# Hymba layer on one core: feed-forward columns interleaved with the output projection, and its input transposed two tiles later

## The chip, the cores and the metric

One core of one Trainium2 chip runs the whole layer in one launch. The metric is the device time of that launch in microseconds (us), as a median of repeated executions. The engines are named as the profile names them: PE (TensorE, matmuls; PEld its weight loads), DVE (VectorE), ACT (ScalarE), POOL (GpSimd) and SP (SyncE, which here only issues DMAs; SPq in the rows). SBUF is the on-chip memory, PSUM holds matmul results, tiles have 128 partitions.

## The reference, cut to what matters

One encoder layer over 2048 positions of width 1024, all in float32. An attention of 8 heads x 64 and a gated unit of 8 groups x 64 read the same normalised input; their outputs stand side by side and go through one output projection. Then comes a feed-forward of hidden width 4096. This part of it is what the change touches:

```python
attn = dilated_attention(q, k, v, rel_bias).reshape(B, S, D_ATTN)
sgu = spatial_gating(jax.nn.gelu(zu), jax.nn.gelu(zv), sgu_ln_g, sgu_ln_b, sgu_w, sgu_b)
mix = jnp.concatenate([attn, sgu], axis=-1) @ w_out
x = x + rms_norm(mix, g_post_mix)
h = rms_norm(x, g_pre_ffn)
f = jnp.square(jax.nn.relu(h @ w_ff1)) @ w_ff2
return x + rms_norm(f, g_post_ffn)
```

## The kernel before

**Precision.** Every matmul operand is split into a high and a low part of a faster float format (the high part by a cast on ACT, the low one as a difference on DVE: `split_sbuf`, L59 and L60, with a scale L56 and L57), and `mm3` makes three matmuls of each product (L84 to L86). So a product of 128x128 by 128x512 is three PE instructions, and each loaded weight costs an ACT and a DVE pass. `piece` loads a 128x512 block of weights on SP's queue into `wraw` and splits it.

**Stages.** Stage 1 (to about 450 us) makes the input projection and the gated unit's inputs. Stage 2 (to about 950 us) is attention, in steps over heads and groups. PE has gaps there, and a generator `gate()` fills them with other work, the *filler*: the rest of the gated unit, and then the half of the output projection that needs only that unit. The filler's results are copied from PSUM to `ot` on ACT (L710) and stored to DRAM as `part`. A plan spreads it: PRE is how much of it (in modelled nanoseconds of PE time) runs ahead of the first step, POST how much stays behind the last, the rest goes in proportion to what the steps leave free. At its last tile the filler loads and splits the eight pieces `c.wo` of `w_out` that the other half of the projection needs. The last `values` of attention are added to DRAM (`od`) by POOL's queue, and a head's denominators are stored as `rd`. At the stage's end the PE and ACT order is pinned to the order in which the code was written (`in_order`); on the other engines a scheduler may move instructions.

**Stage 3** has three loops.
- The output projection, over 16 tiles of 128 positions. `operand(i)` loads `fa` from `od` (L892) and `fr` from `rd` (L895, two loads), multiplies them on POOL (L898) and splits the product into `mh` and `ml`. `rest(i)` loads `r` from `part` (L905) and `xt` from `x` (L907). PE makes 2 x 4 x 3 = 24 matmuls into two PSUM tiles `mo`, DVE adds them to `r` (L936). `post` is a norm and the residual: Square on ACT with a sum (`jk`, L851), two POOL steps for the root (L90, L91), DVE times `gmix` (L912), DVE plus `xt` (L913), a store of `r` to `x1d` on ACT's queue (L914). For the first eight tiles `prep`, one tile behind, norms the new `r` again: Square, two POOL steps, a scaling in place on ACT (L863), eight PE transposes `tp` (L870), and the split of `tp` into `hh` and `hl` (L75, L76). Operands are made two tiles ahead, `rest` one; `r` has three buffers, `xt` two.
- The feed-forward, over two halves of 8 tiles and 8 groups of 512 hidden columns each: `ff1` makes 192 matmuls `f` (4 columns blocks of 128, 8 blocks of the inner dimension, 2 halves of 512 positions, 3 for the precision), Relu on ACT, the square on POOL, a split to `fh` and `fl`; `ff2` makes 192 matmuls `g`, whose sums go to `acc`. The first group's weights are loaded in the last projection tile.
- The output, after the last group of a half: the final norm with `gpost`, the residual from `x1d`, the store.

Memory is handed out in pools, from the left and from the right side of SBUF. A pool that is opened after another one was closed gets its addresses, and its first writers wait for the last readers and writers of what lay there.

## Time and profile before

| | us |
|---|---|
| median of 3 runs | 2513.27 |
| lowest, highest | 2506.41, 2519.23 |
| profiled execution | 2515.86 |
| its span | 2514.0 |
| PE busy in the span | 2390.3 (95%) |
| DVE busy | 1063.1 (42%) |
| ACT busy | 934.9 (37%) |
| POOL busy | 471.2 (19%) |

The span is what the profile shows, from the first instruction to the last; the execution is longer by what lies around it. Busy shares are means over all stages. The page's slices cut the span in 40 equal parts of 62.9 us; each digit is the busy share in tenths, and the row of PE reads `7999999988899996799999999999999999999998`. Slices 16 and 17 (6 and 7, about 943 to 1069 us) are where stage 2 ends and the projection runs. In rows of the timeline the brackets say how long the engine was idle before the instruction and what released it.

### The profile page before, as it was taken

The numbers are of one execution on the slowest core, as the hardware profiler recorded it, in microseconds if no ns is written. First come the engines' busy times: TensorE is split into PE (matmuls) and PEld (weight loads), VectorE is DVE, ScalarE is ACT, GpSimd is POOL, SyncE is SP. The second block draws the span as 40 slices with busy tenths as digits, with TensorE's granted clock in tenths as the row PEclk, the third lists the DMA queues.
The fourth block names the chain that finished last, engine by engine and source line by source line (L and its number), as shares of the span: only waits on it lengthen the run. The fifth ranks groups of instructions, "written<-read, shape, count | busy, mean of one in ns | idle before, by whom it ended". The sixth has DMA issues, their size and how long they took to land.

```text
span 2514.0 us, 31489 instructions
## 1 busy us (share of the span) xinstructions
PE 2390.3 (95%) x11591; PEld 2000.0 (80%) x11591; DVE 1063.1 (42%) x2246; ACT 934.9 (37%) x2053; POOL 471.2 (19%) x521
## 2 busy tenths in 40 slices
PE   7999999988899996799999999999999999999998
PEld 6787888878788885678888888888788888888887
DVE  5433523566766644551322322333722333233226
ACT  4424322366766673433221221123533122212213
POOL 4103103533222222420100110011211001001101
PEclk9999999989999998899999999999999999999999
DMA  7646365878777567761111111111611121111113
GB/s 269 215 138 201 130 189 159 203 175 195 202 175 173 142 153 204 231 232 59 51 47 38 56 47 49 51 51 59 201 59 51 34 67 46 48 42 51 51 43 125
DMA packets 222077, 296.13 MB, mean 118 GB/s; under 512 B 37089, under 2 KB 128740, under 8 KB 218852
## 3 DMA queue, kind: packets, MB, share of 16 engines
q1 hardware_dynamic: 214724, 273.15, 37.4%
q10 hardware_dynamic: 4640, 16.79, 1.7%
q0 software_dynamic: 2560, 4.20, 1.2%
q8 instruction: 91, 1.49, 0.2%
q14 instruction: 62, 0.51, 0.1%
HBM read 216.04 MB, written 82.74 MB: 119 GB/s over the span
## 4 chain that ended last, share of the span: by engine, by line
PE 75%; DMA 12%; DVE 4%; ACT 3%; issue 1%; POOL 1%; SPq 1%; DVEq 0%; ACTq 0%; POOLq 0%
PE f L84 10%; PE f L85 10%; PE f L86 10%; PE g L86 8%; PE g L84 8%; PE g L85 8%; PE mm L84 4%; PE mm L86 4%; PE mm L85 4%; DMA v<-vd 2%; DMA r<-part 2%; PE t L588 2%; PE o L617 1%; PE o L616 1%; PE s L508 1%
## 5 line engine op out<-in xcount | busy, mean ns | idle before, releaser
L85 PE MATMUL f<-hh,wl 128*128 128x512 f32 x1024 | 399.4, 390 | 2.2 <-DVE wl L57 2.2
L86 PE MATMUL f<-hh,wh 128*128 128x512 f32 x1024 | 399.4, 390 | 0.0
L84 PE MATMUL g<-wl,fh 128*128 128x512 f32 x1024 | 399.4, 390 | 0.0
L84 PE MATMUL f<-hl,wh 128*128 128x512 f32 x1024 | 399.2, 390 | 0.0
L86 PE MATMUL g<-wh,fh 128*128 128x512 f32 x1024 | 398.9, 390 | 0.0
L85 PE MATMUL g<-wh,fl 128*128 128x512 f32 x1024 | 398.8, 390 | 0.0
L979 POOL TENSOR_TENSOR sq<-sq 128x512 f32<-128x512 f32 x128 | 131.9, 1051 | 1161.2 <-ACT sq L978 1161.2
L56 ACT ACTIVATE wh<-wraw,gain 128x512 fp32r<-128x512 f32 x200 | 143.3, 724 | 505.8 <-PE g L86 423.3
L57 DVE SCALAR_TENSOR_TENSOR wl<-wraw,gain,wh 128x512 fp32r<-128x512 f32 x200 | 158.0, 797 | 268.5 <-ACT wh L56 265.6
L60 DVE TENSOR_TENSOR fl<-sq,fh 128x512 fp32r<-128x512 f32 x128 | 99.3, 776 | 394.9 <-ACT fh L59 385.9
L85 PEld LDWEIGHTS f<-hh,wl 128*128 128x128 f32 x1024 | 192.6, 188 | 42.6 <-DVE wl L57 2.6
L84 PEld LDWEIGHTS f<-hl,wh 128*128 128x128 f32 x1024 | 192.7, 188 | 40.0
L86 PEld LDWEIGHTS f<-hh,wh 128*128 128x128 f32 x1024 | 192.6, 188 | 39.9
L86 PEld LDWEIGHTS g<-wh,fh 128*128 128x128 f32 x1024 | 192.3, 188 | 39.8
L85 PEld LDWEIGHTS g<-wh,fl 128*128 128x128 f32 x1024 | 192.3, 188 | 39.6
L84 PEld LDWEIGHTS g<-wl,fh 128*128 128x128 f32 x1024 | 192.3, 188 | 39.6
L1006 DVE TENSOR_TENSOR acc<-g,acc 128x512 f32<-128x512 f32 x192 | 127.2, 688 | 165.1 <-PE g L86 165.1
L978 ACT ACTIVATE sq<-f 128x512 f32<-128x512 f32 x128 | 74.8, 597 | 290.5 <-PE f L86 283.3
L577 ACT ACTIVATE p<-p,m 128x256 f32<-128x256 f32 (+2 forms) x384 | 173.8, 458 | 23.7 <-DVE m L549 23.7
L60 DVE TENSOR_TENSOR wl<-wraw,wh 128x512 fp32r<-128x512 f32 x144 | 100.5, 698 | 175.1 <-ACT wh L59 173.8
L59 ACT CAST wh<-wraw 128x512 fp32r<-128x512 f32 x144 | 89.5, 622 | 186.1 <-PE f L86 172.6
L525 DVE CUSTOM_DVE_ANT_0 p<-s,bias 128x256 f32<-128x256 f32 (+2 forms) x384 | 121.1, 356 | 44.2 <-PE s L509 30.5
(156 smaller groups left out, 4170.7 us busy)
## 6 DMA issues: line engine op xcount, KB each, us to landing
wraw<-in_w_ff_dram SPq DMA_DIRECT2D x256, 256.0 KB, 2.7
wraw<-in_w_in_dram SPq DMA_DIRECT2D x72, 256.0 KB, 3.0
xt<-in_x_dram SPq DMA_DIRECT2D x32, 512.0 KB, 5.6
v<-vd SPq DMA_DIRECT2D x40, 256.0 KB, 6.3
v<-vd SPq DMA_DIRECT2D x8, 1088.0 KB, 7.9
hd<-ht ACTq DMA_DIRECT2D x16, 512.0 KB, 5.1
vd<-vt SPq DMA_DIRECT2D x16, 512.0 KB, 3.1
qd<-e SPq DMA_DIRECT2D x32, 256.0 KB, 2.8
```

The costliest lines, as they stand in the source:

```text
L56: nc.scalar.activation(hi, src, AF.Copy, scale=scale)
L57: nc.vector.scalar_tensor_tensor(lo, src, scale, f32(hi), ALU.mult, ALU.subtract)
L59: nc.scalar.copy(hi, src)
L60: nc.vector.tensor_tensor(lo, src, f32(hi), ALU.subtract)
L84: nc.tensor.matmul(out, lhsT=lh, rhs=rl, start=start, stop=False)
L85: nc.tensor.matmul(out, lhsT=ll, rhs=rh, start=False, stop=False)
L86: nc.tensor.matmul(out, lhsT=lh, rhs=rh, start=False, stop=stop)
L525: nc.vector.tensor_tensor_reduce(po, so, bo, -1.0, 1e38, ALU.add, ALU.min, o.nm[:, br, cc:cc + 1])
L577: nc.scalar.activation(p[:, at + lo:at + hi], p[:, at + lo:at + hi], AF.Exp, bias=o.m[:, br, cc:cc + 1], scale=-1.0, accum_out=o.dn[:, br, ...
L978: nc.scalar.activation(sq, b, AF.Relu)
L979: nc.gpsimd.tensor_tensor(sq, sq, sq, ALU.mult)
L1006: nc.vector.tensor_tensor(av, b, av, ALU.add)
```

## The change

Six things change together.

1. POST goes from 4 to 14 modelled us: more of the filler runs behind the last attention step, less of it between the steps.
2. The second norm of a tile (`normed`) writes its result over `xt`, the buffer of the residual input, and not over `r`, which is being stored. Its transposes (`turned`) come two tiles later instead of one. `r` and `xt` have four buffers each, `rest` runs two tiles ahead, and `r` lies on the right side.
3. The first 512 hidden columns of the feed-forward are made for the first half of the positions from weights in pieces of 128x256 (`first`), in units of 256 columns (`ff1_unit`). The unit for columns 0 to 255 is done in two parts, by positions: 0 to 511 between the `mo` matmuls of tiles 6 to 9, 512 to 1023 between those of tiles 10 to 12. A step is six matmuls; a tile has the number of steps in `steps`. The unit for columns 256 to 511 comes behind the loop.
4. `gmix` and `gpost` share one buffer, `gpost` is loaded behind the loop. The right side's first pool (`s3o`) now holds the pieces `w1h` and `w1l`.
5. `fh` and `fl` have 2 + 2 buffers in two pools and not 5, and `y`, `xp` and `acc` lie on the right side.
6. The list `late`, which put the last three `post` behind the loop, goes.

```diff
-        PRE, POST = 8 * 1000.0, 4 * 1000.0
+        PRE, POST = 8 * 1000.0, 14 * 1000.0
...
-        def normed(x1):
+        def normed(x1, out):
             rs = meansq(x1)
-            nc.scalar.activation(x1, x1, AF.Copy, scale=rs)
+            nc.scalar.activation(out, x1, AF.Copy, scale=rs)
...
+        fpa = ctx.enter_context(tc.tile_pool(name="s3f", bufs=2))
+
+        def ff1_unit(h, ws, c0, es, fs, pool):
+
+            hh, hl = h
+            bs = [pm.tile([P, 512], F32, name=f"f{m}", tag="mm3") for m in range(2 * len(es))]
+            for kc in range(8):
+                wh, wl = ws[kc]
+                for m, b in enumerate(bs):
+                    k, e = divmod(m, len(es))
+                    cs = slice(c0 + k * P, c0 + (k + 1) * P)
+                    ts = slice(es[e] * 512, (es[e] + 1) * 512)
+                    mm3(nc, b, wh[:, cs], wl[:, cs], hh[:, kc, ts], hl[:, kc, ts], kc == 0, kc == 7)
+                yield
+            for k in range(2):
+                if len(fs) == k:
+                    fs.append(tuple(pool.tile([P, 1024], F32R, name=x, tag=x) for x in ("fh", "fl")))
+                fh, fl = fs[k]
+                for e in range(len(es)):
+                    ts = slice(es[e] * 512, (es[e] + 1) * 512)
+                    sq = wk.tile([P, 512], F32, name="sq", tag="sq")
+                    nc.scalar.activation(sq, bs[k * len(es) + e], AF.Relu)
+                    nc.gpsimd.tensor_tensor(sq, sq, sq, ALU.mult)
+                    split_sbuf(nc, sq, fh[:, ts], fl[:, ts])
...
-            op = octx.enter_context(tc.tile_pool(name="s3o", bufs=1, side="right"))
-            om = octx.enter_context(tc.tile_pool(name="s3m", bufs=3, side="right"))
-            orp = octx.enter_context(tc.tile_pool(name="s3r", bufs=3))
-            gmix = bcast_row(nc, op, a["g_post_mix"][0:1], D, "gmix")
+            op = octx.enter_context(tc.tile_pool(name="s3o", bufs=8, side="right"))
+            rctx = octx.enter_context(ExitStack())
+            om = rctx.enter_context(tc.tile_pool(name="s3m", bufs=3, side="right"))
+            orp = rctx.enter_context(tc.tile_pool(name="s3r", bufs=4, side="right"))
+            gmix = bcast_row(nc, cst, a["g_post_mix"][0:1], D, "gmix", "gain")
+
+            def first(kc, pr):
+
+                raw = wk.tile([P, 512], F32, name="wraw", tag="wraw", bufs=c.nraw)[:, 0:256]
+                nc.sync.dma_start(raw, w1[kc * P:(kc + 1) * P, pr * 256:(pr + 1) * 256])
+                wh = op.tile([P, 256], F32R, name="w1h", tag="w1h")
+                wl = op.tile([P, 256], F32R, name="w1l", tag="w1l")
+                split_sbuf(nc, raw, wh, wl, c.gffn[:, kc:kc + 1])
+                return wh, wl
...
-            ahead, behind = 2, 1
-            late = []
+            ahead, near, behind = 2, 2, 2
             ops = [operand(i) for i in range(ahead)]
-            rx = [rest(0)]
-            old = []
+            rx = [rest(i) for i in range(near)]
+            old, wa, wb, fs0 = [], [], [], []
             for i in range(16):
                 if i + ahead < 16:
                     ops.append(operand(i + ahead))
-                if i + 1 < 16:
-                    rx.append(rest(i + 1))
+                if 1 <= i < 5:
+                    wa += [first(kc, 0) for kc in range(2 * i - 2, 2 * i)]
                 (mh, ml), (r, xt) = ops.pop(0), rx.pop(0)
+                if i in (6, 10):
+                    unit = ff1_unit(h, wa, 0, (i // 10,), fs0, fpa)
+                steps = {6: 3, 7: 3, 8: 2, 9: 1, 10: 3, 11: 3, 12: 3}.get(i, 0)
                 for n in range(2):
...
                     nc.vector.tensor_tensor(r[:, ns], b, r[:, ns], ALU.add)
-                late.append((i, r, xt))
-                if i < 13:
-                    post(*late.pop())
-                if len(old) == behind:
-                    prep(*old.pop(0))
+                    for _ in range((steps + 1 - n) // 2):
+                        next(unit, None)
+                if len(old) == behind or i == 9:
+                    turned(*old.pop(0)[1:])
+                if i + near < 16:
+                    rx.append(rest(i + near))
+                if 0 < i <= 8:
+                    normed(*old[-1][:2])
+                post(i, r, xt)
                 if i < 8:
-                    old.append((r, h[0], h[1], i))
-            for x in late:
-                post(*x)
-
+                    old.append((r, xt, h[0], h[1], i))
+                if i >= 13:
+                    wb += [first(kc, 1) for kc in range(len(wb), (2, 5, 8)[i - 13])]
+            rctx.close()
+            v0 = load2(0)
+            fpb = ctx.enter_context(tc.tile_pool(name="s3g", bufs=2))
+            fs1 = []
+            for _ in ff1_unit(h, wb, 0, (0, 1), fs1, fpb):
+                pass
```

**SP at the seam between stage 2 and the projection.** `od<-acc` and `od<-av` are the last head's attention outputs, `part<-ot` the filler's stores, `fa<-od` the projection's operands; what stands behind "waits" are the counters that must have moved first. Before:

```order
L633 DMA od<-acc 64x512 [waits DMAHW3_49,DVE_49]
L892 DMA fa<-od 128x4x128 [waits DMAHW4_49,DMASW4_49,DMASW0_49]
L892 DMA fa<-od 128x4x128 [waits DMAHW5_49]
L711 DMA part<-ot 128x512 [waits DMAHW6_49,Activation_49]
L892 DMA fa<-od 128x4x128 [waits DMAHW7_49]
L633 DMA od<-av 64x512 [waits DMAHW0_49,DVE_49]
L711 DMA part<-ot 128x512 [waits DMAHW2_49,Activation_49]
```

And after (`wraw<-in_w_ff_dram 128x256` are loads of the new pieces of the feed-forward's weights):

```order
L913 DMA wraw<-in_w_ff_dram 128x256 [waits DMAHW2_49,DVE_49]
L711 DMA part<-ot 128x512 [waits Activation_49]
L913 DMA wraw<-in_w_ff_dram 128x256 [waits DMAHW6_49,DMAHW3_49,DVE_49]
L913 DMA wraw<-in_w_ff_dram 128x256 [waits DMAHW7_49,DMAHW4_49,DVE_49]
L913 DMA wraw<-in_w_ff_dram 128x256 [waits DMAHW5_49,DMAHW0_49,DVE_49]
L924 DMA fa<-od 128x4x128 [waits DMASW4_49,DMAHW2_49,DMASW0_49,PE_49]
L927 DMA fr<-rd 64x4x128 x2
L924 DMA fa<-od 128x4x128 [waits DMAHW1_49]
```

The first `fa` load has moved from among the last stores of attention to behind the filler's last store of `part` and three loads that wait for DVE; it now waits for PE (the filler's last matmul) and for the landing of that store too.

**ACT in the loop, at the scaling of a normed tile.** `jk` is Square, `hh<-tp` the high part of a transposed tile, `mh<-fa` that of an operand. Before:

```order
L851 ACTIVATE jk_10297,ms_10298<-r 128x1024 [waits DMAHW7_49,DVE_49]
L851 ACTIVATE jk_10306,ms_10307<-r 128x1024 [waits Activation_49]
L59 CAST mh<-fa 128x512 [waits PE_49]
L863 ACTIVATE r<-r,rs_10309 128x1024 [waits DMAHW5_49,Activation_49,Pool_49]
L914 DMA x1d_9947<-r 128x1024 [waits DMAHW4_49,DVE_49]
L75 CAST hh_9951<-tp_10313 128x4x128 [waits PE_49]
L75 CAST hh_9951<-tp_10320 128x4x128 [waits PE_49]
```

After:

```order
L59 CAST mh<-fa 128x512 [waits PE_49,Pool_49]
L857 ACTIVATE xt_10033<-r,rs_10269 128x1024 [waits Pool_49]
L850 ACTIVATE jk_10273,ms_10274<-r 128x1024 [waits DMAHW5_49,Activation_49]
L75 CAST hh_9949<-tp_10332 128x4x128 [waits PE_49]
L75 CAST hh_9949<-tp_10339 128x4x128 [waits PE_49]
L946 DMA x1d_9947<-r 128x1024 [waits DMAHW5_49,DVE_49]
L850 ACTIVATE jk_10350,ms_10351<-r 128x1024 [waits Activation_49]
```

The scaling waits for POOL alone, no longer for a DMA (the store of `r`), and writes `xt`.

**PE in the loop, at the transposes of a tile.** Before, in the middle of a later tile's `mo` matmuls:

```order
L84 MATMUL mo<-wl,mh 128x512
L85 MATMUL mo<-wh,ml 128x512
L870 MATMUL tp_10313<-ident,r 128x128 [waits DVE_49,Activation_49]
L870 MATMUL tp_10313<-ident,r 128x128 x3
L870 MATMUL tp_10320<-ident,r 128x128 [waits DVE_49]
L870 MATMUL tp_10320<-ident,r 128x128 x3
L86 MATMUL mo<-wh,mh 128x512
```

After, at tile 6:

```order
L86 MATMUL mo<-wh,mh 128x512
L864 MATMUL tp_10404<-ident,xt_10096 128x128 [waits DVE_49,Activation_49]
L864 MATMUL tp_10404<-ident,xt_10096 128x128 x3
L864 MATMUL tp_10411<-ident,xt_10096 128x128 [waits DVE_49]
L864 MATMUL tp_10411<-ident,xt_10096 128x128 x3
L84 MATMUL f_10462<-hl_9950,w1h 128x512 [waits DVE_49]
L85 MATMUL f_10462<-hh_9949,w1l 128x512 [waits Activation_49]
L86 MATMUL f_10462<-hh_9949,w1h 128x512
```

The transposes read `xt`, and matmuls `f` of the feed-forward stand behind them, among the projection's.

## Rows read from the trace of the kernel before

**Rows 1.** Windows: us, busy per engine (instructions), PE clock, DMA share, GB/s.

```profile
450.00:950.00 500.00, 449.16 (x2965) 400.54 (x2963) 314.20 (x1124) 327.43 (x1038) 159.52 (x160) 0.94 0.73 178
960.00:1100.00 140.00, 112.24 (x453) 89.04 (x454) 79.23 (x94) 56.73 (x92) 50.65 (x62) 0.88 0.76 228
1120.00:1300.00 180.00, 180.00 (x796) 149.10 (x795) 47.19 (x67) 53.41 (x88) 20.57 (x20) 1.00 0.15 47
```

**Rows 2.** Waits of PE from 450 to 1300: us in total, times, longest.

```profile
PE tp L870 <- ACT r L863: 24.2, 7, 9.7
PE o L616 <- DMA v<-vd: 16.7, 14, 3.3
...
PE f L85 <- DVE wl L57: 2.2, 1, 2.2
```

**Rows 3.** Timeline of PE: start, us, instruction, idle before it and releaser.

```profile
961.31 0.79 PE L84 MATMUL mo<-wl,mh 128*128 128x512 f32 x1 [12.17 <-ACT mh L59]
...
967.16 0.39 PE L85 MATMUL mo<-wh,ml 128*128 128x512 f32 x1
...
991.04 1.97 PE L870 MATMUL tp<-ident,r 128*128 128x128 f32 x8 [9.66 <-ACT r L863]
...
1021.96 1.09 PE L870 MATMUL tp<-ident,r 128*128 128x128 f32 x8 [0.69 <-ACT r L863]
1022.81 0.48 PE L86 MATMUL mo<-wh,mh 128*128 128x512 f32 x1
```

**Rows 4.** Tile `g`: count, ns least/median/most, first and last start.

```profile
L84 PE MATMUL g<-wl,fh x1024: 388/389/482, 1143.3 to 2504.7; 128*128 128x512 f32 x171
```

**Rows 5.** Groups, 960 to 1100: busy, mean ns, idle before and its releasers.

```profile
L851 ACT ACTIVATE jk<-r 128x1024 bf16<-128x1024 f32 x23 | 24.3, 1058 | 29.8 <-DVE r L936 29.1 <-ACT mh L59 0.6
L898 POOL TENSOR_TENSOR fa<-fa,fr 128x512 f32<-128x512 f32 x16 | 23.0, 1435 | 62.1 <-DMA fa<-od 23.2 <-DMA fr<-rd 23.0 <-PE mo L86 10.0
L936 DVE TENSOR_TENSOR r<-mo,r 128x512 f32<-128x512 f32 x30 | 19.9, 686 | 23.5 <-DMA r<-part 21.2 <-PE mo L86 2.3
L91 POOL TENSOR_TENSOR rs<-rs,mhalf 128x1 f32<-128x1 f32 x23 | 18.3, 796 | 1.9
L912 DVE SCALAR_TENSOR_TENSOR r<-r,rs,gmix 128x1024 f32<-128x1024 f32 x14 | 18.0, 1284 | 29.5 <-POOL rs L91 29.5
L913 DVE TENSOR_TENSOR r<-r,xt 128x1024 f32<-128x1024 f32 x14 | 17.1, 1218 | 0.1
L60 DVE TENSOR_TENSOR ml<-fa,mh 128x512 fp32r<-128x512 f32 x16 | 14.2, 885 | 8.9 <-ACT mh L59 8.6
...
L90 POOL TENSOR_SCALAR rs<-ms 128x1 f32<-128x1 f32 x23 | 10.0, 436 | 31.3 <-ACT jk L851 30.6
...
L863 ACT ACTIVATE r<-r,rs 128x1024 f32<-128x1024 f32 x8 | 9.2, 1148 | 28.5 <-POOL rs L91 18.2 <-DMA x1d<-r 10.3
```

**Rows 6.** Timeline of ACT and POOL at the seam, 949 to 962.

```profile
949.88 0.62 ACT L59 CAST wh<-wraw 128x512 fp32r<-128x512 f32 x1 [3.59 <-DMA wraw<-in_w_out_dram]
...
955.71 0.62 ACT L59 CAST wh<-wraw 128x512 fp32r<-128x512 f32 x1 [0.51 <-DMA wraw<-in_w_out_dram]
...
959.36 1.25 POOL L898 TENSOR_TENSOR fa<-fa,fr 128x512 f32<-128x512 f32 x1 [6.14 <-DMA fr<-rd]
...
961.69 0.58 ACT L710 COPY ot<-f 128x512 f32<-128x512 f32 x1
```

**Rows 7.** Tile `part`: us from issue to landing, least/median/most.

```profile
DMA to landing us min/median/max: 2.1/6.3/11.8
```

**Rows 8.** Tile `rd`: its loads (ns), and us from issue to landing.

```profile
L895 SPq DMA_DIRECT2D fr<-rd x32: 574/626/3324, 901.6 to 1046.8; - x32
...
DMA to landing us min/median/max: 4.1/9.1/11.9
```

**Rows 9.** Timeline of POOL and DVE, first projection tile.

```profile
961.63 1.49 POOL L898 TENSOR_TENSOR fa<-fa,fr 128x512 f32<-128x512 f32 x1 [1.02 <-DMA r<-part]
...
961.90 1.76 DVE L60 TENSOR_TENSOR wl<-wraw,wh 128x512 fp32r<-128x512 f32 x1
```

63 lines of the change are left out of this document (19 added, 44 removed).

## The prediction

> **What bounds the kernel now.** The page's slices come first: TensorE's row is all eights and nines but for a few, so the change can win only where it stands, and the windows say where that is [rows 1]. In the 180 us from 1120 it is busy for all of them at a clock of 1.00; in the 140 us from 960, which hold the output projection, for 112.2, and the clock is 0.88, while the DMA engines are busy for 0.76 of the time, as against 0.15. The waits of TensorE [rows 2] put a name to the loss: 24.2 us in seven pieces in front of the transposes (`tp`, L870), all for ScalarE's scaling of `r` (L863), and 2.2 us for the first weights of the feed-forward; the timeline adds 12.17 us once, in front of the first projection matmul [rows 3].
>
> **The projection as it is.** From the first `mo` at 961.31 [rows 3] to the first `g` at 1143.3 [rows 4] are 182.0 us. At full clock one matmul starts at 967.16, and 59 later the last ahead of the longest idle ends at 991.04 - 9.66 = 981.38 [rows 3], so starts 0.39 earlier at 980.99: 13.83 / 59 = 0.2344 us each. The stretch holds 16 x 24 `mo` and 192 `f` matmuls, 576 x 0.2344 = 135.0, and eight groups of eight transposes; the warm one takes 0.85 to the next matmul (1021.96 to 1022.81) [rows 3], so 6.8. Work: 141.8 us. Waits: 24.2 + 2.2 = 26.4. The other 13.8 us are work at the lower clock. One sees it at the eight transposes behind the idle 9.66, which take 1.97, where those behind an idle of 0.69 take 1.09 [rows 3]. The clock falls when TensorE has stood, and stays down for a while after: a microsecond of waiting costs about half a one more (13.8 / 26.4).
>
> **A, transposes two tiles later, columns between.** Today the tile's chain is: DVE adds (L936, L912, L913), Square on ScalarE, two POOL steps, the store of x1, and only then the scaling in place, which also waited 10.3 us in all for that store (`DMA x1d<-r`) [rows 5]. TensorE stands for it one tile later, after 5.6 us of matmuls. The change lets the scaling write another buffer, so the wait on the store goes, and puts 48 + 48 `f` matmuls (2 x 11.2 us) and one more tile between. Work is the same 141.8: 96 matmuls move in among the tiles, 96 stay behind them. What is late next is the chain itself. Its loop from tile to tile, in the program order of after: Square of the finished tile and of the new one on ScalarE (2 x 1.06), the pair of POOL steps 0.44 + 0.80, the two DVE passes 1.28 + 1.22 [rows 5]: 5.9 us. Into it fall the product on POOL, 1.44, and the split `ml` on DVE, 0.89: 8.2 us; with two adds L936 (2 x 0.69) it is 9.6. TensorE needs 5.6 for a tile's `mo`, 6.5 with transposes, and 4.2 or 2.8 more in tiles 6 to 8, where three or two steps of six `f` stand too. So the chain falls behind in the first six tiles and catches up later. Tile 3 is scaled at about 5.6 + 4 x 8.2 + 3.5 = 41.9 (3.5 is its own Square, POOL pair and Copy, 1.06 + 1.24 + 1.15), and TensorE reaches its transposes at 6 x 5.6 + 3 x 0.85 = 36.2: 6 us of idle, gathered over tiles 0 to 3; later tiles are no worse (tile 7: 75 against 73 + 6). Add 2 for the cold start and, at half a microsecond each, 3 for the idle: 141.8 + 6 + 2 + 3 = **153**, a gain of 29. Bounds: 144 (no idle, cold start alone), and 166: at 9.6 a tile the idle is 11.3, its clock 6, and 5 for operands that land late, `r<-part` being already what DVE waits for, 21.2 us at L936 [rows 5].
>
> **B, the seam between the stages.** Now the last filler matmul ends at 949.14 and TensorE then idles 12.17 us [rows 3]; the last link is `fr`, which lands for the POOL product at 959.36 [rows 6]; with `mh` behind it that is 1.95 ahead of the first matmul. `fa` had been loaded long before. In the new SP order the first `fa` load waits for that last filler matmul, and for the last store of `part`: the right side's pool has grown, and `fa` now lies on the filler's buffers. That store waits for ScalarE's `ot`, which stands behind eight splits of `w_out`; before, `ot` ran at 961.69, 12.6 after the filler's end, and hurt nobody. From 949.88 to 955.71 four splits start [rows 6], 1.94 apart; eight of them from the start of the last filler tile (24 x 0.234 = 5.6 before its end) take 7 x 1.94 + 0.62 = 14.2, so `ot` comes 8.6 after it. Then 0.6 for the copy, 3 for the store (landing 2.1 at least, 6.3 in the middle) [rows 7], 1.7 for SP's issues (`fr` 0.63 each, twice, and `fa` somewhat less), 5 for the operands (`rd`'s issues land in 4.1 at least, 9.1 in the middle) [rows 8], and 1.95 for product and `mh`: 20.9, call it 21. **Cost 9.** Bounds: 0.6 + 2.1 + 1.7 + 4.1 + 1.95 = 10.5, say 11, if `ot` isn't late at all, a gain of 1; and 12.6 + 6.3 + 1.7 + 11 + 1.95 = 33.5, a loss of 21, if it is as late as now and landings are slow. I take the working's own value, between them, since it goes by the pace that the splits show; `ot` can come later, as splits of w1 mix in, and earlier, as the last head's exchange is over by then.
>
> **C, filler moved out of attention.** POST grows by 10 modelled us: 48 filler matmuls more, 48 x 0.2344 = 11.2 us, run after the last attention value and so lengthen the tail. They leave attention, where TensorE is busy 449 of 500 us [rows 1] and most matmul time comes straight back; but its waits on `v` (16.7, in 14 pieces) [rows 2] are tied to loads, and a thinner filler gives those back as idle. I take 3 us not returned; the bounds are 0 and 11.2.
>
> **The rest at nothing.** The weights of the first 512 columns are now 16 loads and splits of half the width in place of eight: the same bytes, hidden behind the filler tail and tiles 13 to 15 (if that cover fails, it is the 2.2 again) [rows 2]. Four `fh`/`fl` buffers, not five: TensorE, with no idle from 1120 to 1300 [rows 1], has passed the matmuls that read a buffer before the next group writes it. `gpost` in one buffer with `gmix`, `y` and `xp` on the other side: used late, no wait on TensorE's path.
>
> **Sum.** -29 + 9 + 3 = -17. The profiled execution took 2515.9 (its span 2514.0 and 1.9 around it), which gives 2498.7 or so; it lies 2.6 above the median 2513.3 of the three, so the forecast for a median is **2496**.
>
> **Rivals.**
> *The seam is free.* `ot` isn't late (the w1 splits wait, the last filler's copies go ahead) and the filler comes back whole: -29 - 1 + 1 for a colder start, 2513.3 - 29, 2484. For it: ScalarE stood idle before the splits, waiting for their loads [rows 6], so there is room for copies. Against it: the order puts `ot` behind all eight.
> *The seam eats it.* Nothing of the 11.2 comes back and the seam is 25: -29 + 13 + 11 = -5, 2508. For it: DMA queues are busy at 0.76 just there [rows 1], which makes landings long.
> *Slower: VectorE and GpSimd block each other in the chain.* At 961.90 a split `wl` took 1.76 while a POOL product of 1.49 ran from 961.63 on [rows 9]; the like split `ml` has a mean of 0.89 [rows 5], so a block costs 0.87. Two per tile make the loop 9.9, three 10.8. Then tile 7 is scaled at 5.6 + 8 x 10.8 + 3.5 = 95.5 against TensorE's 10 x 5.6 + 7 x 0.85 + 11.2 = 73.4: 22 us of idle for 6, 16 more and half of that again for the clock, 2520. At 10.2 it is 17.5 of idle, 17 more with the clock, 2513: the point from which this is slower than before. Against it: the means of rows 5 hold such blocks already.
> The Trainium skill, "SBUF — State Buffer", Who interferes with whom, says that a VectorE instruction with two inputs in SBUF contends with a GpSimd instruction that reads SBUF, and that the one that comes second is blocked for the whole of the other; the 1.76 agrees with it [rows 9]. By that rule alone both passes of the chain (L912, L913) and the split could each meet a POOL step, which is this rival's three blocks, 2520.
> *The change doesn't do what it says:* transposes still stand for their input (the DVE order puts the adds late); projection 166, so -16 + 9 + 3 = -4, 2509.
>
> **How the numbers follow.** Forecast 0.43 (2490 to 2507), seam free 0.26 (2478 to 2490), seam eats it 0.18 (2504 to 2514), slower 0.10, no effect 0.03. What a measurement of this kernel can tell from no change is about 0.5%, 12.6 us: faster is below 2500.7, slower above 2525.8. Faster: all of "free" and 0.30 of the forecast, 0.56. Slower: the blocking case where the seam goes to its upper end as well (2520 + 12), 0.06. Same: 0.38. The range 2478 to 2514 leaves out the blocking case and a little of the ends of A.
>
> **What would show it.** A: no `tp` wait on ScalarE over 4 us, none on a store of x1, 150 to 157 us from first `mo` to first `g`. B: the wait of the first `mo` near 21, released through `fa<-od` and not `fr<-rd`. C: attention to its last value shorter by about 8. Wrong: a loop over 10 us a tile, DVE passes over 2 us, or the wait in front of the first `mo` under 12.

## The result, and the profile after

The changed kernel is slower: a median of 2530.84 us in 9 runs against 2514.93 in 9 runs of the kernel before, a ratio of 1.0086 with a 95% interval of 1.0069 to 1.0103. The forecast was 2496 with a range of 2478 to 2514. At 1.0086 the loss is some 21 us; the medians alone differ by 15.9. In the experiments below, two runs in a slow state are left out, one of e5 (5570 us) and one of e11 (4475).

The profiled execution of the changed kernel took 2517.12 (span 2515.3), the fastest of its nine; the other eight lie between 2525 and 2539. So its trace shows the stages but not the whole loss. What it lacks can be named. Attention is measured here from the first start of the row `s<-kl,qs` (scores of one kind of head; those of the other, `qg`, begin some 30 us earlier) to the last start of the rows of `o`:

```profile
L508 PE MATMUL s<-kl,qs x128: 251/284/563, 452.0 to 852.8; 128*128 128x256 f32 x112, 128*128 128x192 f32 x16
...
L617 PE MATMUL o<-th,v x448: 270/280/420, 486.1 to 917.1; 128*128 128x128 f32 x86, 128*128 128x256 f32 x64
```

That is 917.1 - 452.0 = 465.1 us, and the six kernels below whose operand loads stand at the same place have 471.8 to 477.8. So some 10 us of the loss are probably hidden by that one attention stage.

The waits of TensorE from 940 to 1300 in the changed kernel (us in total, times, longest), which answer to [rows 2]:

```profile
PE mo L84 <- ACT mh L59: 23.5, 2, 23.2
PE tp L864 <- ACT xt L857: 21.3, 6, 4.9
PE f L84 <- DVE hl L76: 6.6, 2, 4.7
```

And its timeline of TensorE, which answers to [rows 3], with the row of `g` that answers to [rows 4]:

```profile
956.71 0.79 PE L84 MATMUL mo<-wl,mh 128*128 128x512 f32 x1 [23.17 <-ACT mh L59]
...
982.79 1.97 PE L864 MATMUL tp<-ident,xt 128*128 128x128 f32 x8 [4.87 <-ACT xt L857]
...
1008.82 1.97 PE L864 MATMUL tp<-ident,xt 128*128 128x128 f32 x8 [4.14 <-ACT xt L857]
1022.39 1.97 PE L864 MATMUL tp<-ident,xt 128*128 128x128 f32 x8 [3.93 <-ACT xt L857]
...
L84 PE MATMUL g<-wl,fh x1024: 388/389/481, 1144.9 to 2506.1; 128*128 128x512 f32 x171
```

From the first `mo` to the first `g` are now 1144.9 - 956.7 = 188.2 us, six more than the 182.0 of before, where 153 were forecast. The waits for the scaled tile have hardly shrunk, 21.3 for 24.2 us; the longest is 4.9 and not 9.7, but there are 6.6 more for `hl`. The seam has grown from 12.17 to 23.17.

The groups from 950 to 1120, which answer to [rows 5] (busy, mean ns, idle before it and what ended it):

```profile
L850 ACT ACTIVATE jk<-r 128x1024 bf16<-128x1024 f32 x23 | 24.2, 1054 | 38.8 <-DVE r L945 27.5 <-DVE r L966 9.1 <-issue 1.4
L930 POOL TENSOR_TENSOR fa<-fa,fr 128x512 f32<-128x512 f32 x16 | 21.7, 1359 | 98.0 <-DMA fr<-rd 61.2 <-DMA fa<-od 27.2 <-DMA x1d<-r 6.5
L945 DVE TENSOR_TENSOR r<-r,xt 128x1024 f32<-128x1024 f32 x14 | 19.4, 1385 | 0.1
L944 DVE SCALAR_TENSOR_TENSOR r<-r,rs,gmix 128x1024 f32<-128x1024 f32 x14 | 18.7, 1338 | 48.4 <-POOL rs L91 41.1 <-ACT sq L895 7.3
L91 POOL TENSOR_TENSOR rs<-rs,mhalf 128x1 f32<-128x1 f32 x23 | 13.1, 568 | 1.9
L857 ACT ACTIVATE xt<-r,rs 128x1024 f32<-128x1024 f32 x8 | 9.2, 1146 | 21.4 <-POOL rs L91 21.4
```

Three things stand here. The wait of the scaling on the store of x1 is gone, as the change wanted: L857 waits for POOL's `rs` alone, and all of its 21.4. The instructions are not much longer than before: each pass of the chain on DVE and ACT is within 0.17 us of its mean in [rows 5], and POOL's step L91 is shorter, 0.57 us for 0.80. And POOL stood idle for 98.0 us in front of the product of `fa` and `fr`, 27.6 of them at the seam, so 70 in the loop with 61 for the loads. Before, the 62.1 of [rows 5] hold the 6.1 in front of the first product [rows 6], so the loop had 56 with 40 for the loads.

How the two are tied shows in the timeline of POOL and ScalarE at one tile, with TensorE's row that waits for it:

```profile
990.57 1.06 ACT L850 ACTIVATE jk<-r 128x1024 bf16<-128x1024 f32 x1
...
992.47 1.28 POOL L930 TENSOR_TENSOR fa<-fa,fr 128x512 f32<-128x512 f32 x1 [6.55 <-DMA fr<-rd]
993.84 0.22 POOL L90 TENSOR_SCALAR rs<-ms 128x1 f32<-128x1 f32 x1
994.14 0.57 POOL L91 TENSOR_TENSOR rs<-rs,mhalf 128x1 f32<-128x1 f32 x1
...
994.74 1.15 ACT L857 ACTIVATE xt<-r,rs 128x1024 f32<-128x1024 f32 x1 [3.02 <-POOL rs L91]
...
995.95 1.10 PE L864 MATMUL tp<-ident,xt 128*128 128x128 f32 x8 [2.68 <-ACT xt L857]
```

POOL took the steps in the order in which they stand. Those of the root stand behind a product for a later tile, and that product waits 6.55 us for `fr`. ScalarE, and behind it TensorE, are put down to `rs` and to `xt`, but what they wait for is a load.

### The profile page after: what moved, and what is told of

Same layout as the page of the kernel before. It is cut to its first block, busy times and chain, and to the rows that moved or that the text cites. A ratio compares the mean times of both kernels' runs of the same rounds, so it can differ in the third digit from the quotient of the medians.

```text
span 2515.3 us, 31521 instructions
## 1 busy us (share of the span) xinstructions
PE 2390.8 (95%) x11591; PEld 1996.9 (79%) x11591; DVE 1062.6 (42%) x2254; ACT 935.3 (37%) x2061; POOL 457.2 (18%) x521
## 4 chain that ended last, share of the span: by engine, by line
PE 64%; DMA 7%; DVE 3%; ACT 3%; POOL 1%; issue 1%; SPq 1%; ACTq 0%; POOLq 0%; DVEq 0%
PE f L84 10%; PE f L85 10%; PE f L86 10%; PE g L84 8%; PE g L85 8%; PE g L86 8%; PE t L588 2%; PE o L617 1%; PE o L616 1%; DMA v<-vd 1%; ACT p L577 1%; PE s L508 1%; DMA fa<-od 1%; PE s L509 1%; DMA fr<-rd 1%
## 5 line engine op out<-in xcount | busy, mean ns | idle before, releaser
L85 PE MATMUL f<-hh,wl 128*128 128x512 f32 x960 | 373.6, 389 | 0.0
L84 PE MATMUL f<-hl,wh 128*128 128x512 f32 x960 | 373.6, 389 | 0.0
L86 PE MATMUL f<-hh,wh 128*128 128x512 f32 x960 | 373.6, 389 | 0.0
L56 ACT ACTIVATE wh<-wraw,gain 128x512 fp32r<-128x512 f32 x192 | 137.8, 724 | 503.3 <-PE g L86 421.8
L57 DVE SCALAR_TENSOR_TENSOR wl<-wraw,gain,wh 128x512 fp32r<-128x512 f32 x192 | 151.7, 796 | 268.9 <-ACT wh L56 268.2
L85 PEld LDWEIGHTS f<-hh,wl 128*128 128x128 f32 x960 | 180.2, 188 | 37.4
L84 PEld LDWEIGHTS f<-hl,wh 128*128 128x128 f32 x960 | 180.2, 188 | 37.4
L86 PEld LDWEIGHTS f<-hh,wh 128*128 128x128 f32 x960 | 180.2, 188 | 37.4
L577 ACT ACTIVATE p<-p,m 128x256 f32<-128x256 f32 (+2 forms) x384 | 174.0, 459 | 22.8 <-DVE m L549 22.8
L60 DVE TENSOR_TENSOR wl<-wraw,wh 128x512 fp32r<-128x512 f32 x144 | 99.3, 691 | 172.1 <-ACT wh L59 170.8
```

Source lines behind the costliest of these rows:

```text
L56: nc.scalar.activation(hi, src, AF.Copy, scale=scale)
L57: nc.vector.scalar_tensor_tensor(lo, src, scale, f32(hi), ALU.mult, ALU.subtract)
L60: nc.vector.tensor_tensor(lo, src, f32(hi), ALU.subtract)
L84: nc.tensor.matmul(out, lhsT=lh, rhs=rl, start=start, stop=False)
L85: nc.tensor.matmul(out, lhsT=ll, rhs=rh, start=False, stop=False)
L86: nc.tensor.matmul(out, lhsT=lh, rhs=rh, start=False, stop=stop)
```

## The experiments

Time ratios are against the kernel before, run beside. Of each profile the table gives three stages: attention (measured as above), the seam (idle in front of the first `mo`), the projection (first `mo` to first `g`). 'Early' or 'late' is where the first loads of `fa` stand in SP's order: among attention's last stores, or behind the filler.

| kernel | median | ratio, 95% | attention | `fa` | seam | projection |
|---|---|---|---|---|---|---|
| before | 2514.9 | 1 | 489.5 | early | 12.2 | 182.0 |
| e16, before again | 2510.5 | 1.0004 (0.9988 to 1.0020) | 481.6 | early | 11.7 | 183.0 |
| changed | 2530.8 | 1.0086 (1.0069 to 1.0103) | 465.1 | late | 23.2 | 188.2 |
| e1, POST 4 | 2522.7 | 1.0052 (1.0038 to 1.0067) | 474.2 | late | 25.7 | 190.6 |
| e2, POST 14 alone | 2524.6 | 1.0060 (1.0047 to 1.0074) | 481.7 | early | 6.1 | 191.9 |
| e3, old place of `fa` | 2526.1 | 1.0074 (1.0057 to 1.0091) | 483.1 | early | 6.9 | 201.3 |
| e4, no columns between | 2526.3 | 1.0067 (1.0053 to 1.0080) | 475.7 | late | 25.0 | 184.4 |
| e5, one `fr` load | 2504.3 | 0.9961 (0.9945 to 0.9978) | 471.8 | late | 26.7 | 157.5 |
| e6, loads on POOL's queue | 2552.7 | 1.0166 (1.0147 to 1.0186) | 477.8 | late | 27.0 | 208.5 |
| e7, POST 4 and old place | 2516.3 | 1.0013 (0.9998 to 1.0027) | 479.5 | early | 11.7 | 192.9 |
| e8, loop part alone | 2523.7 | 1.0048 (1.0031 to 1.0065) | 485.8 | early | 12.6 | 195.4 |
| e9, changed, pairs | 2516.4 | 1.0033 (1.0021 to 1.0045) | 475.7 | late | 26.4 | 173.6 |
| e10, before, pairs | 2494.7 | 0.9948 (0.9929 to 0.9967) | 478.0 | early | 11.8 | 172.1 |
| e11, e7 with pairs | 2499.8 | 0.9959 (0.9946 to 0.9971) | 482.9 | early | 12.6 | 171.8 |
| e12, before, `fr` in fours | 2495.2 | 0.9948 (0.9932 to 0.9964) | 474.3 | late | 28.3 | 160.9 |
| e13, e12 with the old seam | 2493.9 | 0.9942 (0.9923 to 0.9961) | 479.2 | early | 12.5 | 166.9 |
| e14, e8 with pairs | 2505.3 | 0.9982 (0.9967 to 0.9997) | 480.9 | early | 15.1 | 178.4 |
| e15, e2 with pairs | 2503.5 | 0.9967 (0.9950 to 0.9985) | 480.8 | early | 3.8 | 176.3 |
| e17, e14, norms swapped | 2501.9 | 0.9964 (0.9948 to 0.9980) | 484.8 | early | 15.5 | 174.0 |
| e18, e11, norms swapped | 2491.7 | 0.9921 (0.9900 to 0.9942) | 486.4 | early | 13.6 | 167.1 |

### The parts one by one: POST, the place of `fa`, the columns

**e1**, POST back to 4 in the changed kernel:

```diff
-        PRE, POST = 8 * 1000.0, 14 * 1000.0
+        PRE, POST = 8 * 1000.0, 4 * 1000.0
```

> The changed kernel with POST back at 4: only the amount of filler behind attention is undone. Theory 'the filler comes back whole' (my term C near 0): time within 4 us of the changed kernel, the last attention value about 11 us later, the idle ahead of the first projection matmul 23 to 28. Rival 'thinner attention is what paid for 15 us in the changed kernel's profile' : the end of the filler moves from 933.5 back to about 949 and the kernel is 10 to 15 us slower than the changed one.

Measured: 0.34% faster than the changed kernel, some 8.5 us, where the first theory had 4 at most and the rival a loss. The last values come 10.5 us later than in the changed kernel's profile, but that is this one profile's short attention: e4 below has the changed kernel's POST, and its attention (475.7) is as long as that of e1 (474.2).

**e2**, the same number alone in the kernel before (4 to 14):

> The kernel before with POST at 14 and nothing else. Operands fa and fr then have about 11 us more to arrive under the filler. Theory 'filler comes back, seam is hidden': idle ahead of the first projection matmul falls from 12.2 to 1 to 4, the time falls by 8 to 11 us. Rival 'the filler doesn't come back': the idle falls as much, attention is not shorter, the time is within 3 us of before.

Measured: 15 us slower than before, which neither theory had. The idle in front of `mo` fell to 6.1, where it is no longer `fr` but the weights that TensorE waits for:

```profile
PE tp L870 <- ACT r L863: 28.7, 7, 10.5
PE mo L84 <- DVE wl L60: 8.4, 4, 6.1
PE f L85 <- DVE wl L57: 3.0, 1, 3.0
```

These are waits of TensorE from 940 to 1200 in e2. Its attention took as long as with all the filler in it:

```profile
L508 PE MATMUL s<-kl,qs x128: 251/284/562, 453.8 to 865.9; 128*128 128x256 f32 x112, 128*128 128x192 f32 x16
...
L617 PE MATMUL o<-th,v x448: 271/280/420, 487.9 to 935.5; 128*128 128x128 f32 x86, 128*128 128x256 f32 x64
```

These are the rows of tiles `s` and `o` in e2: 935.5 - 453.8 = 481.7 us, and e16, with POST at 4, has 481.6. As one kernel's profiles differ by 8 us here (e16 below), the table's means say more: the three early profiles with POST at 14 (e2, e3, e15) have 481.9 us, the ten with POST at 4 have 482.9. Of the 11.2 us of filler about 1 comes back.

**e3**, the place of `fa` alone, and **e7**, both undone:

```diff
+            om = octx.enter_context(tc.tile_pool(name="s3m", bufs=3, side="right"))
             op = octx.enter_context(tc.tile_pool(name="s3o", bufs=8, side="right"))
             rctx = octx.enter_context(ExitStack())
-            om = rctx.enter_context(tc.tile_pool(name="s3m", bufs=3, side="right"))
```

> The changed kernel with the operands' pool opened ahead of the pool of the weight pieces, so that fa lies where it lay before and its first load waits for attention's results alone, not for the filler. Theory 'the seam is a matter of the address': the idle ahead of the first projection matmul falls from 23.2 to 0 to 5, and the kernel is 18 to 23 us faster than the changed one. Rival 'the weights of the projection set the seam': idle stays over 12, gain under 10.

> The changed kernel with both seam parts undone: POST at 4 and the operands' pool on the addresses it had before. What is left of the change is the loop: scaling into the residual's buffer, transposes two tiles later, columns between. Theory 'the loop brings nothing, seam and POST brought the loss': within 5 us of the kernel before, idle ahead of the first projection matmul 9 to 14. Rival 'the loop brings its gain once the seam is as before': 12 to 29 us faster than before.

Measured: in e3 the seam shrinks from 23.2 to 6.9 (nearly the first theory's 0 to 5) and the time doesn't follow (1.0074): its profile has a projection of 201.3 us, 13 more. That profiled execution took 2533.5, 7 over e3's median, so the 13 are at the high end. In e7 the seam is that of before, 11.7, and the time too (1.0013), with a projection of 192.9. So with POST and the seam undone, what is left of the change brings nothing, and the forecast's 29 us are not merely covered by the seam.

**e4**, no columns between the tiles (`steps` is zero, both parts of the unit run behind the loop):

> The changed kernel with all feed-forward columns behind the projection loop, none between its tiles. Theory 'the loop is paced by loads and by what stands behind them, PE has idle time to fill': PE waits more in the loop (transposes 25 to 45 us in all, against 21.3), and the kernel is 8 to 20 us slower than the changed one. Rival 'the interleaved matmuls bring nothing, as they stand behind late transposes': within 4 us.

Measured: 1.0067, no slower than the changed kernel's 1.0086, and the projection with all its columns takes 184.4 us, not more than 188.2. The rival holds: in this loop, columns that stand behind transposes that wait fill nothing. (The best version below shows them, with the rest of the change, in a loop that waits less.)

### What the loop waits for

**e5** loads the denominators for the first tile alone and uses them for all:

```diff
-                fr = om.tile([P, 4, P], F32, name="fr", tag="fr")
...
+                if i == 0:
+                    fr1.append(om.tile([P, 4, P], F32, name="fr", tag="fr", bufs=1))
+                    rv = c.rd[:, sl].rearrange("(k e) s -> e k s", e=2)
+                    for e in range(2):
+                        nc.sync.dma_start(fr1[0][e * DH:(e + 1) * DH], rv[e].partition_broadcast(DH))
+                fr = fr1[0]
```

> The changed kernel with the denominators fr loaded for the first tile alone and used for all sixteen (so the values of the other tiles are not those of the reference): 30 of the 48 operand loads' transfers go, 128 KB each. Theory 'the loop is paced by operand loads that land late, with the norm's POOL steps queued behind the product': first mo to first g falls from 188 to 155 to 168, the transposes' waits from 21 to under 9, the kernel is 18 to 30 us faster than the changed one. Rival 'the norm's own chain (Squares, POOL steps, DVE passes) sets the pace': projection stays over 180, gain under 6 us.

Measured: 1.0086 falls to 0.9961, some 31 us, and the projection to 157.5. TensorE's waits for the scaled tile are all but gone (940 to 1200):

```profile
PE mo L84 <- ACT mh L59: 26.7, 1, 26.7
PE f L84 <- DVE hl L76: 6.8, 2, 6.1
PE tp L864 <- ACT xt L857: 2.1, 2, 2.0
```

Each of the loads that went is small, 128 KB. How much of the engines' time they took shows in the DMA views of the projection's loop, first the changed kernel's (956.7 to 1122; queue: packets, MB, share of 16 engines; then issues, KB each, median us to landing), then that of e5 (965.4 to 1099.7):

```profile
q1 hardware_dynamic: 20604, 24.54, 56.4%
q10 hardware_dynamic: 1990, 7.29, 10.8%
...
fa<-od SPq DMA_DIRECT2D x14, 256.0 KB, 9.5
fr<-rd SPq DMA_DIRECT2D x28, 128.0 KB, 9.4
```

```profile
q1 hardware_dynamic: 12163, 19.49, 47.9%
...
fa<-od SPq DMA_DIRECT2D x13, 256.0 KB, 2.8
```

The share times 16 engines times the stretch is 1492 us of engine time in the one and 1029 in the other. So 8441 packets and 5.05 MB cost 462 us of engine time, 55 ns a packet and about 11 GB/s an engine. 7168 of these packets are the 28 `fr` loads in rows of 512 B (128 floats); the rest is what the longer stretch holds more of `r`, `fa` and weights. With these loads gone, `fa` lands in 2.8 us and not in 9.5.

It is not the short rows as such. The rows of `fa` are 512 B long too, and in the packet records of e5's trace (size and time of each) its loop holds 6838 packets of 512 B, nearly all `fa`, that took 27.6 ns in the mean: 18.6 GB/s an engine, as against 18.9 for the loads in rows of 4 KB in the same loop. In the changed kernel's loop, with `fa` and `fr`, 14504 packets of 512 B took 42.6 ns, 12.0 GB/s. One thing that sets `fr` apart is that 64 partitions read the same row (`partition_broadcast` above); whether that is the cause was not tried.

**e6** issues `fa` and `fr` from POOL's queue, past SP's loads of `r`, which wait for the store of x1:

> The changed kernel with the loads of fa and fr issued from POOL's queue and not from SP's, where they stand behind loads of r that wait for the store of x1 (39.7 us of waits on SP). Theory 'the wait on SP delays the operand loads': projection 165 to 176, the kernel 8 to 20 us faster than the changed one. Rival 'the transfers themselves are slow, whichever queue issues them': projection 182 to 195, within 6 us of the changed kernel or slower.

Measured: 1.0166, the projection 208.5. That is 20 us slower than the changed kernel, so POOL's queue made it worse. The loads landed sooner after their issue (`fa` in 5.3 us, `fr` in 7.4), and POOL still waited 47 us for them in the loop (971.8 to 1157). As POOL is in the chain itself, this doesn't say how much SP's queue costs.

**e9** and **e10** load `fa` and `fr` for two tiles at a time, rows of 1 KB:

```diff
-                fa = om.tile([P, 4, P], F32, name="fa", tag="fa")
-                fr = om.tile([P, 4, P], F32, name="fr", tag="fr")
...
+                if i % 2 == 0:
+                    sl = slice(i * P, (i + 2) * P)
+                    fa_ = om.tile([P, 4, 2 * P], F32, name="fa", tag="fa", bufs=2)
+                    nc.sync.dma_start(fa_, c.od[:, sl].rearrange("(k p) s -> p k s", p=P))
...
+                fa = far[0][:, :, i % 2 * P:(i % 2 + 1) * P]
+                fr = frr[0][:, :, i % 2 * P:(i % 2 + 1) * P]
```

> The changed kernel with fa and fr loaded for two tiles at a time: the same bytes in rows of 1 KB and not of 512 B, half as many loads. Theory 'small rows make the operand loads slow, and the loop follows them' (without 30 of the fr loads fa landed in 2.8 us and not 9.5, and the projection took 157.5 and not 188.2): projection 162 to 175, 12 to 24 us faster than the changed kernel. Rival 'the bytes count, not the rows': projection 183 to 195, within 5 us of the changed kernel.

> The kernel before with fa and fr loaded for two tiles at a time. Theory 'small rows': the pace of 10.5 us a tile falls to 9 or 9.5 (then the store of x1 sets it), projection 168 to 177, 5 to 14 us faster than before. Rival 'before isn't bound by its operand loads': within 4 us of before.

Measured: the changed kernel falls from 1.0086 to 1.0033 (projection 188.2 to 173.6), the kernel before to 0.9948 (182.0 to 172.1): 13 us each, though the bytes are the same. Both times lie where the first theory had them, and POOL's waits for its loads in the loop shrink from 61 to 18 us in the changed kernel and from 40 to 24 in the one before. These are the lines of e9 (970.7 to 1122) and of e10 (948.1 to 1090):

```profile
POOL fa L939 <- DMA fr<-rd: 9.0, 2, 6.2
POOL fa L939 <- DMA fa<-od: 8.6, 2, 6.0
```

```profile
POOL fa L907 <- DMA fr<-rd: 13.5, 4, 5.0
POOL fa L907 <- DMA fa<-od: 10.1, 3, 4.6
```

The theory's reason does not hold, though. By the packet records of these loops the rows of 1 KB ran no faster by the byte: 80.7 ns each in e9 (12.7 GB/s an engine) and 84.2 in e10 (12.2), against 42.6 ns for 512 B in the changed kernel (12.0) and 37.9 in the one before (13.5). Pairs also halve the number of loads, and their two buffers hold four tiles where three held three. Which of the two gives the 13 us was not tried.

**e12** puts only `fr` in fours (rows of 2 KB), **e13** adds the old seam by loading the first two tiles' `fr` one by one:

> The kernel before with the denominators fr alone loaded for four tiles at a time (rows of 2 KB, a quarter of the loads), fa as it was. Theory 'the many small rows of fr slow every transfer beside them': fa lands in 4 to 6 us and not 8.3, projection 168 to 178, 4 to 14 us faster than before. Rival: within 4 us of before.

> The kernel before with the denominators in fours, but those of the first two tiles loaded one by one into the operands' pool, so that the first loads lie where they lay before and don't wait for the filler's end. e12 took 160.9 us from first mo to first g but stood 28.3 us at the seam. Theory 'the two add': seam 10 to 14, projection 160 to 168, 10 to 16 us faster than e12, some 25 to 31 faster than before. Rival 'an earlier start of the projection is lost in it again' (as with POST in e2): within 5 us of e12.

Measured: e12 has the shortest projection of all that compute the reference's values, 160.9, shorter than forecast, and `fa` lands in 6.6, a little over the forecast; but the larger pool moved `fa` onto the filler's buffers, as in the change, and the seam is 28.3. e13 mends the seam (12.5) and is no faster (0.9942 against 0.9948): attention is 4.9 us longer in its profile, the projection 6.0, and the two together take back 11 of the 16. The rival holds here, and the table shows the one half of it throughout: the thirteen profiles with early `fa` loads have an attention of 478.0 to 489.5 us, the seven with late ones 465.1 to 477.8. e3 beside the changed kernel and e7 beside e1 differ in that place alone, and there too early is longer, 483.1 against 465.1 and 479.5 against 474.2. Early loads stand in SP's queue among attention's last stores and wait for results; that this is how they lengthen attention's end is argued and was not tried by itself, and the two ranges only just don't meet.

### What the loop part costs by itself

**e8** is the kernel before with the scaling into `xt`, the transposes two tiles later, and nothing else of the change but four buffers for `xt`, `fh` and `fl`:

```diff
-            ahead, behind = 2, 1
+            ahead, behind = 2, 2
...
+                if 0 < i <= 8:
+                    normed(*last)
                 if i < 13:
                     post(*late.pop())
-                if len(old) == behind:
-                    prep(*old.pop(0))
+                if len(old) == behind or i == 9:
+                    turned(*old.pop(0))
```

> The kernel before with one part of the change: the scaling writes the residual's buffer (four of them), the transposes come two tiles later, and fh and fl have four buffers as in the changed kernel; no columns between, POST at 4, operands where they were. Theory 'the loop is paced by loads and what is queued behind them, and a later place of the transposes moves the wait, not the pace': within 5 us of before, waits in front of the transposes still 18 to 30. Rival, my term A: projection 182 to 160 to 168, 12 to 22 us faster than before.

Measured: 1.0048, 12 us slower, with a projection of 195.4. Neither theory had a loss. The waits that the change was to end are longer than before:

```profile
PE tp L865 <- ACT xt L858: 37.3, 6, 9.9
...
POOL fa L893 <- DMA fr<-rd: 68.4, 15, 9.5
```

These are TensorE's and POOL's waits of e8 (940 to 1200, and 954.6 to 1102.6). Does the loss vanish with prompt loads? **e14** is e8 with pairs, **e11** the change with its seam mended (e7) and pairs, **e15** is e2 with pairs:

> e8 (scaling into the residual's buffer, transposes two tiles later, nothing else) with operand loads for two tiles at a time. Theory 'late operand loads took it': as fast as e10 or up to 8 us faster, projection 164 to 173. Rival 'the loop part has a cost of its own, its order of the norm's steps': 6 to 14 us slower than e10, projection 178 to 188.

> The changed kernel with POST at 4, the operands' pool on its old addresses and operand loads for two tiles at a time: what is left of the change is its loop, with its loads on time. Theory 'the loop's gain was real and the late loads took it': 12 to 26 us faster than the kernel before, projection 160 to 172. Rival 'bytes, not rows': within 5 us of the kernel before, projection over 185.

> e2 (POST at 14 alone) with operand loads for two tiles at a time. Theory 'late operand loads took it': within 4 us of e10. Rival 'filler moved behind attention doesn't come back': 8 to 16 us slower than e10, as e2 is to before.

Measured: beside e10 (0.9948), the loop part with pairs is at 0.9982, POST with pairs at 0.9967, the mended change at 0.9959. That is 10 us faster than before for the mended change, less than the 12 that its theory had at least. The loads took part of it, but the loop part keeps a cost of its own: e14 lies 11 us behind e10 by the medians and 9 by the ratios, whose intervals just meet. e15 lies 9 and 5 us behind, with intervals that overlap, so with prompt loads a cost of POST is likely and not shown.

For the loop part the diff has a candidate: the second norm of tile i-1 now stands ahead of the first norm of tile i. **e17** swaps the two calls in e14, **e18** in e11 (this is e18 against e11):

```diff
+                post(i, r, xt)
                 if 0 < i <= 8:
                     normed(*old[-1][:2])
-                post(i, r, xt)
```

> e14 with the two calls of a tile swapped: the first norm of tile i, then the second norm of tile i-1, as before the change. Theory 'the order chains the tiles': 8 to 16 us faster than e14, projection 162 to 172, as fast as e10 or faster. Rival 'the later transposes or the residual's buffer cost it': within 4 us of e14.

> e11 (the change with POST at 4, operands' pool on its old addresses, operand loads for two tiles) with the two norms swapped in the same way. Theory 'the order chains the tiles': 8 to 16 us faster than e11, 2485 to 2493, faster than e10 by what the interleaved columns fill, 2 to 9 us. Rival: within 4 us of e11.

The group of Squares in e14, e17, e11 and e18, in that order, each over its own loop (from 952, 958, 955 and 960, to 1100, 1100, 1104 and 1104):

```profile
L851 ACT ACTIVATE jk<-r 128x1024 bf16<-128x1024 f32 x24 | 25.3, 1055 | 50.9 <-DVE r L917 28.7 <-DVE r L940 21.4 <-DMA r<-part 0.5
```

```profile
L851 ACT ACTIVATE jk<-r 128x1024 bf16<-128x1024 f32 x24 | 25.4, 1058 | 20.0 <-DVE r L940 19.9
```

```profile
L850 ACT ACTIVATE jk<-r 128x1024 bf16<-128x1024 f32 x23 | 24.3, 1058 | 25.9 <-DVE r L954 10.7 <-DVE r L975 10.0 <-DVE w1l L57 3.4
```

```profile
L850 ACT ACTIVATE jk<-r 128x1024 bf16<-128x1024 f32 x23 | 24.4, 1061 | 16.8 <-DVE r L975 12.5 <-DMA fr<-rd 3.7 <-ACT mh L59 0.6
```

L917 and L954 are the pass that adds the residual, the last of the tile before; L940 and L975 the one that adds `mo`. With the change's order the Squares wait 28.7 and 10.7 us for the tile before to be finished; with the calls swapped that wait is gone. The time follows in e18, 0.9921 against 0.9959 with intervals apart, where the theory had 8 to 16 us. In e17 it hardly does: 0.9964 against 0.9982, some 4 us, with intervals that overlap, which is the rival's range. So the order chained the tiles, and it cost the mended change 9 us. Of the 11 us of e14 it explains some 4, which is not clear of the noise; what the later transposes and the four buffers cost beside it stays open.

**e16**, the kernel before once more:

> The kernel before, unchanged, for a second profile. If one profile's stages are typical: from first scores to last values 485 to 494 us, projection 179 to 186. If stages vary between executions: either of them off by over 5 us.

Measured: the projection is the same, 183.0; attention is 8 us shorter, 481.6. By this one pair, projections can be compared from one profile to the next, attention only to about 8 us.

**The best version is e18**: 2491.7, 0.9921 (0.9900 to 0.9942), 20 us faster than before. e10, the kernel before with larger loads and nothing else, has 13 to 15 of them, and the two intervals overlap. e18 and e17 have the same place of the transposes, the same loads and the same order of norms; e18 has beside these the rest of the change but for POST and the place of `fa` (the columns between, a fourth buffer for `r`, `rest` a tile earlier), and it is 11 us faster, 0.9921 against 0.9964 with intervals apart. So the rest of the change brings something once the loop waits less; which part of it does was not tried.

## Why the prediction was wrong

**The projection as it is: right.** 182.0 us with 141.8 of work; e16 has 183.0.

**A failed, in two steps of its working.** The first is the loop of 8.2 us. It put the product on POOL at its 1.44 us of work, as though its loads were there, and left the wait for them to the bound. In e5, where 30 of them are not made, eight tiles are scaled between 984.9 and 1043.8, 8.4 us apart, so the chain itself was sized well, and the projection took 157.5 where 153 was forecast. In the changed kernel they are scaled from 981.59 to 1067.01, 12.2 apart, which is the prediction's own sign of being wrong, a loop over 10 us. It could have been read ahead: [rows 5] has 46 us of idle in front of the product for loads (40 in the loop), and the scaling's wait is put down to POOL's `rs` for 18.2 of 28.5 us. The forecast followed the store of x1, the 10.3, and took the rest for work of the chain. The bound of 166 had 5 us for operands that land late; without most of the `fr` loads the projection is 31 us shorter (e5).

The second step is the order of the two norms. The loop of 5.9 us was written down "in the program order of after", with both Squares in it, but was not compared with the order before, where tile i's norm needn't wait for the one before it. e18 shows that this is a cost of the change, 9 us with prompt loads; e17 only points the same way. The sign that did come, no wait on a store of x1, shows that the wait that was removed was not what set the pace.

**B was right in its mechanism and its size, and incomplete.** 23.2 us for 21 forecast, and 25 to 27 in e1, e4, e5, e6 and e9; with the old place of the pool it is 11.7 (e7). The steps are in the changed kernel's timelines of PE, ACT, SP and POOL:

```profile
933.14 0.39 PE L86 MATMUL f<-wh,xh 128*128 128x512 f32 x1
...
942.47 0.58 ACT L710 COPY ot<-f 128x512 f32<-128x512 f32 x1
...
943.08 0.33 SPq L711 DMA_DIRECT2D part<-ot  x1
...
945.45 0.38 SPq L924 DMA_DIRECT2D fa<-od  x1
945.88 1.30 SPq L927 DMA_DIRECT2D fr<-rd  x2
...
954.74 1.26 POOL L930 TENSOR_TENSOR fa<-fa,fr 128x512 f32<-128x512 f32 x1 [27.62 <-DMA fr<-rd]
```

The copy comes 8.9 us after the last filler matmul's end at 933.54 (8.6 forecast), `fa` is issued 2.4 behind the store (3 forecast; loads of weights stand between in the queue, so the wait for the landing isn't seen by itself), the issues take 1.7 (1.7), the operands land 7.6 after them (5), and 2.0 remain to the first `mo` (1.95). Only the sign was named wrongly: the product is released through `fr`, which stands behind `fa` in SP's queue. What was missed is the other side: with the loads out of attention's last stores, attention is some 9 us shorter, by the means of the seven late and the thirteen early profiles in the table (473.5 and 482.6). In e3 the gain at the seam is lost elsewhere.

**C had the right sign and the wrong size.** 3 us not returned were forecast with a bound of 11.2; by the means of the early profiles some 10 stay out (481.9 us with POST at 14, 482.9 with POST at 4). The tail did grow as forecast: from the last values to the first `mo` e2 has 72 matmuls and e16 24. TensorE's 449 busy of 500 us did not make it the limit there. The sign for C, attention shorter by about 8, came (465.1 for 489.5), but by luck: the place of `fa` and the spread between profiles made most of it, and POST about 1 us. What of the 15 us in e2 is beyond some 10 less the 6 that the seam gives back is a projection of 191.9 against 183.0 us; with pairs it is 176.3 against 172.1. Why an earlier filled seam lengthens the projection is left open.

**The sum.** By these sizes: A +6, B +11 and about -9, C +10, together +18, against 16 to 21 measured (medians and ratio).

**The rivals.** The one that ended on the other side had the right place, the norm's chain, and the wrong mechanism. DVE's passes are 1.34 and 1.39 us long, not 2, and so 0.05 and 0.17 us longer than before; the rule of the Trainium skill that was weighed there ("SBUF — State Buffer", Who interferes with whom) can have cost no more than that a pass beyond what it cost before. That the case's 2520 comes nearest to the measured time is luck. "The change doesn't do what it says" is closest, by its 166 and its "transposes still stand for their input", and had a chance of 0.03.

**Range and chances.** The only case with a time clearly over 2514 had a chance of 0.10. The bounds of A stopped at a loop of 9.6 us, though the kernel before ran one of 10.5 (scaled at 989.83 and 1062.99, seven tiles apart).

## What to carry to other kernels

A wait that ends with an engine in the profile is only a first step: ask what that engine had ahead in its queue, and go on until a load or real work ends it; here "TensorE waits for ScalarE" was a 128 KB load three engines away. Before changing the order of a pipeline, measure its pace per tile and compare it with the work of its links: 10.5 us for 8.2 of work says that something outside the chain may set it. Try fewer and larger loads before moving the work that waits for them.

## What the runs showed of the hardware

- Loads in rows of 512 B ran as fast as loads in rows of 4 KB where the `fr` loads were gone: 18.6 and 18.9 GB/s an engine in e5's loop. The Trainium skill, "DMA: Bandwidth & Descriptors", Specifications, gives 512 B as the least transfer for line rate; e5's trace agrees in so far as longer rows were no faster there.
- Loads of one row by 64 partitions (`fr`) went with slow transfers of their own size: with them in the loop packets of 512 B took 42.6 ns in the mean, without them 27.6, and `fa` landed in 9.5 and in 2.8 us. Rows of twice the length did not help by the byte (80.7 and 84.2 ns in e9 and e10).
- TensorE was busy for 90% of attention and yet not its limit: 48 matmuls taken out of it, 11.2 us of work, left its length at 481.9 us by the mean of three profiles, against 482.9 by that of ten.
